# A conditioned decoder layer on one core: u and the spatial gates in token-major seven-product blocks

## The chip, the cores and the metric

The kernel runs on one core of a Trainium2 chip. The core has a matrix engine (PE, with its weight loads shown as PEld), a vector engine (DVE), a scalar engine (ACT), GpSimd (POOL) and a queue engine (SP), and 16 DMA engines that move data between the main memory and the on-chip buffer. Transfers are issued by SP; those that add into their destination are issued by POOL. Results of PE go to PSUM, eight banks of 128 partitions by 512 numbers. The metric is the time of one execution in microseconds of the device, lower is better.

## The reference

One layer works on 512 tokens of 2048 channels. The token matrix is normalised and modulated by a conditioning vector, and one projection gives everything that the two mixers need:

```python
proj = h @ w_in[l]
q_lat, kv_lat, k_rope, z_mla, u, v, z_sgu, g_mla, g_sgu = split_cols(proj, IN_SPLITS)
...
y_mla = causal_mla_attention(q_nope, q_rope, k_nope, k_rope, v_mla) * jax.nn.silu(z_mla)
mixed = jnp.einsum('gts,bnsgd->bntgd', ws, vc) + b_spatial.T[None, None, :, :, None]
y_sgu = u * mixed.reshape(B, S, SGU_WIDTH) * jax.nn.silu(z_sgu)
merged = jax.nn.sigmoid(g_mla) * y_mla + jax.nn.sigmoid(g_sgu) * y_sgu
x = x + gate[:, None] * (merged @ w_out[l])
return rmsnorm(x, final_norm_g)
```

`u`, `v`, `z_mla`, `z_sgu`, `g_mla`, `g_sgu` are 2048 channels wide each, 16 heads (or groups) of 128. In the spatial gating, `v` is normalised, cut into four chunks of 128 tokens, and for each group g multiplied by a lower triangular 128 x 128 matrix over the tokens of a chunk. The product of u, the mix, silu(z_sgu) and sigmoid(g_sgu) is called T below. All arithmetic is fp32.

## The kernel before

**Precision.** Each fp32 operand is split into a high and a low part (`hilo`, line 145: a cast by ACT, a subtraction by DVE), and each product is three matmuls, high by high, low by high, high by low. A weight tile of 128 x 1024 numbers (512 KB) is fetched raw, split, and used from one of three pairs of buffers (w0, w1, w2).

**Order of the stages.** First the latent columns (w1, w2: the low-rank q and kv latents and one 128-column head of z, g and u each), then 1088 of the v columns and one head of z by plain products (the loop over `steps`), then the first 1024 columns of v as a block of seven products (`V7`, 28 slots), then the other heads of z, g, u, s (= z_sgu) and t (= g_sgu) as 38 pairs of heads (`PAIRS`, 266 slots), then attention head by head, then the output projection.

**Seven products.** The product of a token half by a channel half is done after Winograd, with seven products for eight. The token sides are sums of the activations, made once (s1, s2, s4, and one that overwrites half of hh/hl). The weight sides are sums of raw weight tiles: B12 (called kept) plus B11, plus B22, minus B11 ("11b", `v_t3`), plus B21.

- In the *v block* the tokens are stationary and the weights stream, 512 columns at a time, so the result comes out token-major (128 tokens by 512 channels). A slot is one product over a quarter of the channels: 12 matmuls of 512 columns (lines 1422 to 1424). Four weight tiles are kept, and three buffers (raw4, raw5, raw6) take the passing ones in turn. Where sums are made by DVE, it is `v_sum` and `v_t3`; the last four sums (B21) are made by accumulating transfers on POOL's queue (line 901).
- In the *pairs* the weights are stationary and the tokens stream, 256 at a time, and the result is channel-major (128 channels by 512 tokens). A slot is one product over all eight channel tiles: 24 matmuls of 256 columns, or, for two of the seven, 8 of 512 and 8 of 256 (lines 1443 to 1447). Weight tiles are contiguous rows of 4 KB. Of a pair's four sums, DVE makes one and accumulating transfers three (`transfer`, line 722, issued in line 728); DVE makes more in the first and the last pair.

**A slot's order.** `on(s, phase, f)` puts work on slot s, in the order FIRST, EVAC, GATE, SPLIT, BACK, then PE's matmuls, then MISC and LOAD. The weights of slot g are split in slot g - 2. `place` finds, from slot s on, the first with room in DVE's budget, which is written down by `spend`: at most 3.2 us in a slot and 5.566 in two neighbours. Loads are issued in order by SP, accumulations in order by POOL, and each waits there until its buffer is free.

**The spatial mix.** For each group `v_load` fetches v token-major from a scratch in main memory, `sgu_scale` and `sgu_split` scale and split it, and `sgu_mix` multiplies with v stationary and the 256-wide high and low spatial weights streaming (lines 998 and 999), eight matmuls, which gives channel-major results in two banks. `sgu_out` (line 1002) puts in the gain and the broadcast bias and leaves it in the tile `bs[g]`; the pairs' gates (`gate_op`, line 827) then multiply u, s and t into it, and T is stored channel-major, one 256 KB tile a head.

**Other work of the pair stage.** The rotary tables (`rope_make`), the products of the shift with w1 and w2 that correct the early latents (`share`, 52 pieces of 256 KB, two accumulators in turn), and the normalisation of the latents (`lat_sq`, `lat_norm`), which fetches each of ten tiles twice.

**Attention.** `fetch(h)` loads T and the gate g of a head ahead of time. After the scores, the softmax, the transposes of the probabilities (line 1607) and the product with v, `merge_a` (line 1629) multiplies the result by g; its deferred second half adds T and splits the sum. PSUM banks go round in a ring of seven.

Of the kernel before, what the change touches and what calls it, by code (L numbers as in the profile page):

```python
# [20 lines left out]
P = 128  # L21
D = 2048
S = 512
# [40 lines left out]
class Stream:  # L64
# [17 lines left out]
    def dma_to(self, i):  # L82
        i = min(i, len(self.src) - 1 if self.limit is None else self.limit)
        while self.n_dma <= i:
# [7 lines left out]
            (self.first if k == 0 else self.nc.sync).dma_start(t[:, :n], ap)  # L92
# [29 lines left out]
def trunk_layer(ctx, tc, xT, xn, c, vecs, pos, wada, w1, w2, wv, wv3, wv4, wh, wh15, wq, wqr, wk, wvv, wo, wsT, bsp, gfin, out,  # L122
# [91 lines left out]
    gate_row = scratch("gate_row", [KC, P])  # L214
    cact_d = scratch("cact_d", [1, D])
# [7 lines left out]
    out_d = {t: [scratch(f"{t}_d{i}", [8, P, S]) for i in range(2)] for t in "gt"}  # L223

    lat = [nt(latp.p, [P, S], F32, f"lat{i}") for i in range(13)]
# [14 lines left out]
    g2 = [ws.add(w2[k], 640) for k in range(KC)]  # L240
# [9 lines left out]
    for cg, i in steps:  # L250
        if cg == "z":
            gb.append(ws.add(wh[H - 2, 0, i], GW))
# [236 lines left out]
    def half_of(tags, j):  # L489

        if j % 2 == 0:
            halves_[tags, j // 2] = nt(latp.p, [P, S], F32, tags[j // 2])
# [41 lines left out]
    def evac_v(n, cg, ps):  # L534
# [6 lines left out]
        else:  # L541
            t = nt(latp.p, [P, S], F32, "lat10" if n == 2 else "lat11" if cg == 1 else "lat6")
# [16 lines left out]
    def v_kept(i):  # L559
        p, tag = kept_at[i]  # L560
        kept[i] = nt(p(), [P, GW], F32, tag)
        DMA.dma_start(kept[i], wv[1][i])

    def v_pass(what, i):

        n = len(passing)
        t = passing[what, i] = nt(c1[0].p, [P, GW], F32, ("raw6", "raw4", "raw5")[n % 3])
        g, half = {"11": (0, 0), "11b": (0, 0), "21": (0, 4), "22": (1, 4)}[what]
        DMA.dma_start(t, wv[g][half + i])

    def v_sum(what, i):
        tt(kept[i], kept[i], passing[what, i], ALU.add)

    def v_t3(i):
        t = passing["11b", i]
        tt(t, kept[i], t, ALU.subtract)

    def v_split(g):
        p, i = V7[g]
        t = kept[i] if p in (6, 2, 4) else passing[{1: "11", 7: "22", 3: "11b", 5: "21"}[p], i]  # L580
        pl, tag = [(wp, "w1"), (wp, "w0"), (c1[0].p, "w2")][g % 3]
        vparts[g] = hi, lo = nt(pl, [P, GW], F32R, tag + "h"), nt(pl, [P, GW], F32R, tag + "l")
        hilo(hi, lo, t)

    for at_, f, *a in ((20, v_pass, "11", 0), (21, v_kept, 0), (22, v_pass, "11", 1), (23, v_kept, 1), (24, v_kept, 2),
# [1300 lines left out]
```

## Time and profile before

| | |
|---|---|
| median of three runs | 1594.26 us (1593.98 to 1595.37) |
| the profiled execution | span 1591.8 us from the first to the last instruction; no other time is given for it, and the median stands 2.5 us above it |
| granted PE clock, mean | 0.998 |
| v block | 259.49 to 335.78 us |
| pairs | from 335.78 us to about 1100 us |
| DMA | 335.35 MB, 211 GB/s on the mean |
| POOL's accumulating transfers | 60.30 MB, 21.6% of 16 engines' span |

A row of groups has the line, the engine, the operation, output and inputs, the shape, the count, and then the busy time, the mean of one in ns and the idle time before. A row of a timeline has the start, the duration, the engine and the operation, and in brackets the idle time before it and what ended it. A matmul's duration holds its passage through the array, so the pace of PE is read from starts and not from durations. A row of windows has the stretch, its length, busy time of PE, PEld, DVE, ACT and POOL with counts, the granted clock, the busy share of the DMA engines and GB/s. A row of a queue has packets, MB and the share of 16 engines' time.

### The profile page before, as it was taken

How to read it: one execution, taken by the hardware profiler on the slowest of the kernel's cores; microseconds unless marked ns; L12 is line 12 of the kernel's file. 1: busy time of each engine (PE TensorE's matmuls, PEld its weight loads, DVE VectorE, ACT ScalarE, POOL GpSimd, SP SyncE). 2: the span in 40 equal slices, each digit the busy share in tenths (PEclk: the TensorE clock that was granted, in tenths of full speed). 3: DMA queues.
4: the chain of work that ended last, by engine and by line, in shares of the span. 5: the costliest groups of instructions: out<-in, count | busy, mean ns of one | idle time of the engine just before them, and what ended most of it. 6: DMA issues, size and time to landing. Idle time of an engine off the chain costs nothing.

```text
span 1591.8 us, 25847 instructions
## 1 busy us (share of the span) xinstructions
PE 1579.7 (99%) x10107; PEld 1446.7 (91%) x10107; DVE 1225.3 (77%) x1831; ACT 766.4 (48%) x1271; POOL 108.4 (7%) x132
## 2 busy tenths in 40 slices
PE   9999999999999999999999999999999999999997
PEld 8888999889999999999999999999888898888886
DVE  8989788767877887787877777777788887866763
ACT  4443335555555454454545645645655555532332
POOL 0000000000111111111111111112000000000000
PEclk9999999999999999999999999999999999999999
DMA  9978566678799998889988879889422322339822
GB/s 384 358 290 317 199 185 216 179 221 223 204 235 244 244 260 227 219 241 237 232 210 241 232 205 265 221 216 224 147 83 87 102 90 86 97 135 387 289 88 106
DMA packets 124781, 335.35 MB, mean 211 GB/s; under 512 B 14298, under 2 KB 35826, under 8 KB 117874
## 3 DMA queue, kind: packets, MB, share of 16 engines
q1 hardware_dynamic: 106066, 272.88, 48.8%
q0 software_dynamic: 18448, 60.30, 21.6%
q8 instruction: 79, 1.29, 0.3%
q10 hardware_dynamic: 144, 0.52, 0.1%
q14 instruction: 44, 0.35, 0.1%
HBM read 309.45 MB, written 24.20 MB: 210 GB/s over the span
## 4 chain that ended last, share of the span: by engine, by line
PE 93%; DMA 2%; DVE 2%; ACT 1%; issue 1%; SPq 0%; DVEq 0%; ACTq 0%
PE ps L1447 15%; PE ps L142 14%; PE ps L143 14%; PE ps L141 14%; PE ps L1445 10%; PE ps L1446 10%; PE ps L1443 8%; PE ps L1424 2%; PE ps L1423 2%; PE ps L1422 2%; PE ps L1607 1%; PE ps L1570 1%; PE ps L1571 1%; DMA wsr<-in_wsT 1%; PE ps L998 1%
## 5 line engine op out<-in xcount | busy, mean ns | idle before, releaser
L1445 PE MATMUL ps<-hh,w2h 128*128 128x256 f32 x408 | 115.9, 284 | 0.0
L1445 PE MATMUL ps<-hh,w0h 128*128 128x256 f32 x408 | 115.6, 283 | 0.0
L1446 PE MATMUL ps<-hl,w2h 128*128 128x256 f32 x408 | 115.4, 283 | 0.0
L1446 PE MATMUL ps<-hl,w0h 128*128 128x256 f32 x408 | 115.4, 283 | 0.0
L1447 PE MATMUL ps<-hh,w0l 128*128 128x256 f32 x408 | 115.4, 283 | 0.0
L1447 PE MATMUL ps<-hh,w2l 128*128 128x256 f32 x408 | 115.4, 283 | 0.0
L1445 PE MATMUL ps<-hh,w1h 128*128 128x256 f32 x400 | 113.6, 284 | 0.0
L1446 PE MATMUL ps<-hl,w1h 128*128 128x256 f32 x400 | 113.2, 283 | 0.0
L1447 PE MATMUL ps<-hh,w1l 128*128 128x256 f32 x400 | 113.1, 283 | 0.0
L129 DVE TENSOR_TENSOR lat<-ps,lat 128x256 f32<-128x256 f32 (+2 forms) x202 | 97.1, 485 | 19.7 <-ACT lat L146 8.3
L132 DVE SCALAR_TENSOR_TENSOR wada<-wada,cact 128x2048 f32<-128x2048 f32 x47 | 107.2, 2281 | 4.7 <-DMA wada<-in_wada 4.7
L129 DVE TENSOR_TENSOR w2l<-raw,w2h 128x1024 fp32r<-128x1024 f32 x63 | 77.1, 1223 | 34.8 <-ACT w2h L748 30.9
L111 ACT CAST w1h<-wraw 128x1024 fp32r<-128x1024 f32 (+3 forms) x65 | 54.6, 841 | 99.0 <-PE ps L143 42.3
L111 ACT CAST w0h<-wraw 128x1024 fp32r<-128x1024 f32 (+3 forms) x66 | 60.4, 915 | 80.6 <-PE ps L143 29.9
L112 DVE TENSOR_TENSOR w0l<-wraw,w0h 128x1024 fp32r<-128x1024 f32 (+3 forms) x66 | 69.1, 1047 | 29.1 <-ACT w0h L111 28.9
L728 POOL DMA_DIRECT2D wraw<-in_wh x67 | 59.3, 939 | 448.3 <-DVE w0l L129 168.8
L141 PE MATMUL ps<-hh,w1h 128*128 128x512 f32 x226 | 89.7, 397 | 0.0
L129 DVE TENSOR_TENSOR w0l<-wraw,w0h 128x1024 fp32r<-128x1024 f32 x46 | 56.3, 1224 | 42.4 <-ACT w0h L748 40.0
L142 PE MATMUL ps<-hl,w1h 128*128 128x512 f32 x226 | 88.3, 391 | 0.5 <-DVE hl L132 0.5
L143 PE MATMUL ps<-hh,w1l 128*128 128x512 f32 x226 | 88.1, 390 | 0.0
L129 DVE TENSOR_TENSOR w1l<-raw,w1h 128x1024 fp32r<-128x1024 f32 x51 | 62.4, 1224 | 26.7 <-ACT w1h L748 23.5
L112 DVE TENSOR_TENSOR w1l<-wraw,w1h 128x1024 fp32r<-128x1024 f32 (+3 forms) x65 | 62.4, 960 | 26.0 <-ACT w1h L111 25.0
(410 smaller groups left out, 5298.3 us busy)
## 6 DMA issues: line engine op xcount, KB each, us to landing
raw<-in_wh SPq DMA_DIRECT2D x105, 512.0 KB, 6.3
wada<-in_wada SPq DMA_DIRECT2D x47, 1024.0 KB, 7.3
wraw<-in_wh POOLq DMA_DIRECT2D x67, 512.0 KB, 7.1
wraw<-in_wh SPq DMA_DIRECT2D x45, 512.0 KB, 7.2
raw<-in_wh POOLq DMA_DIRECT2D x42, 512.0 KB, 8.4
wraw<-in_wo SPq DMA_DIRECT2D x32, 512.0 KB, 5.0
half<-in_w SPq DMA_DIRECT2D x35, 256.0 KB, 5.7
raw<-in_wv SPq DMA_DIRECT2D x17, 512.0 KB, 3.9
```

The source lines that it names most:

```text
L111: self.nc.scalar.copy(hi[:, :n], raw[:, :n])
L112: self.nc.vector.tensor_tensor(out=lo[:, :n], in0=raw[:, :n], in1=hi[:, :n].bitcast(F32), op=ALU.subtract)
L129: DVE.tensor_tensor(out=out, in0=in0, in1=in1, op=op)
L132: DVE.scalar_tensor_tensor(out=out, in0=in0, scalar=scalar, in1=in1, op0=op0, op1=op1, **kw)
L141: PE.matmul(ps, ah, bh, start=start, stop=False)
L142: PE.matmul(ps, ah, bl, start=False, stop=False)
L143: PE.matmul(ps, al, bh, start=False, stop=stop)
L728: q_.dma_start(t, wh[h, n, q // 10 - 1], **eng)
L1443: PE.matmul(open_bank[k, "z"], wH[:, sl], both_parts[p](c), start=st, stop=False, skip_group_check=True)
L1445: PE.matmul(ps, wH[:, sl], xh, start=st, stop=False, skip_group_check=True)
L1446: PE.matmul(ps, wH[:, sl], xl, start=False, stop=False, skip_group_check=True)
L1447: PE.matmul(ps, wL[:, sl], xh, start=False, stop=sp, skip_group_check=True)
```

## The change

The 24 pairs that hold u, s and t become six blocks of the v block's form, 28 slots each, between the v block and the pairs; 14 pairs of z and g are left. A block has two column groups of 512 channels, four heads of one kind each.

- **Blocks and their weights.** `BLOCKS` lists them. `fill` gathers a weight tile from four heads: 256 numbers (1 KB) of each head's row, so a tile is 128 x 4 pieces of 1 KB; for the group with head 15 a second transfer brings that head from another array in pieces of 512 B. PE reads the moving operand as four runs of 128 (`p (h k w) -> p k h w`). Per block four tiles are kept and 16 pass; the B22 and the B21 sums are accumulating transfers, eight a block (also in the v block), B11 and B12 minus B11 are made by DVE. The next block's first tiles are fetched in the last nine slots of the one before.
- **Evacuation.** `t_copy`, `t_sub`, `t_add` move a quarter (two tiles of 128 x 512) at a time into six double tiles d0 to d5 that take the place of the single tiles lat0 to lat11. `squash` then applies Silu (s) or Sigmoid (t) to 1024 numbers a partition in one ACT instruction; `t_gate` multiplies it into u.
- **Mix.** v is multiplied by the gain (a row broadcast from main memory), the spatial weight is stationary, v streams: three matmuls of 512 columns into one bank, token-major. `sgu_out` is one operation for each token half, adding the bias per token and multiplying into u.
- **T** is stored token-major, eight tiles of 512 KB, fetched in pieces of 512 B, and turned in attention by four transposes a head (`turn`), with the add moved from the deferred half of the merge to the front.
- **Budget.** DVE's budget in `place` is 3.0 and 5.25 us in the blocks.
- **Moved.** The rotary tables, the shares and the mixes begin in block 1 instead of pair 0. The shares run one accumulator after another, each stored and fetched again before it is turned. Latent tiles are fetched once. The head of z that was done by plain products is now in w2's granules and head 14 of g is done by plain products in its place.

```diff
-PAIRS = [((t, h), (t, h + 1)) for h in range(0, 14, 2) for t in TYPES]
-PAIRS[:0] = [(("g", 14), ("u", 14))]
-PAIRS += [((t, 14), (t, 15)) for t in "st"]
+PAIRS = [((t, h), (t, h + 1)) for h in range(0, 14, 2) for t in "zg"]
+BLOCKS = [("v", 0, "v", 1)]
+for c_ in (0, 2):
+    BLOCKS += [("u", c_, "s", c_), ("t", c_, "u", c_ + 1), ("s", c_ + 1, "t", c_ + 1)]
...
+    def fill(q_, t, b, g, i, **kw):
+        ty, c = BLOCKS[b][2 * g:2 * g + 2]
+        if ty == "v":
+            q_.dma_start(t, wv[c][i], **kw)
+            return
+        n, half, o = TYPES.index(ty), i // 4, i % 4 * 2 * P
+        t = t.rearrange("p (h x) -> p h x", h=4)
+        hs = slice(4 * c, min(4 * c + 4, H - 1))
+        q_.dma_start(t[:, :hs.stop - hs.start], wh[hs, n, half][:, :, o:o + 2 * P].rearrange("h p x -> p h x"), **kw)
+        if hs.stop < 4 * c + 4:
+            src = w2[2 * i:2 * i + 2][:, :, S:].rearrange("k p w -> p k w")
+            if ty != "u":
+                src = wh15[i].rearrange("p (k t w) -> p k t w", k=2, t=2)[:, :, n - 3]
+            q_.dma_start(t[:, 3].rearrange("p (k w) -> p k w", k=2), src, **kw)
...
+    def v_add(b, g, i):
+        fill(nc.gpsimd, kept[b, i], b, g, 4 + i, accum_op=ALU.add)
...
-            return own > 3.2 or own + max(a, b) > 5.566
+            return own > (3.2 if s >= 0 else 3.0) or own + max(a, b) > (5.566 if s >= 0 else 5.25)
...
+    n_v = len(V7)
+    at_block = [n_v * (b - len(BLOCKS)) for b in range(len(BLOCKS))]
+    for b, V in enumerate(at_block):
...
+        sums_ = [(V - 2 + 2 * i, GATE, v_sum, b, "11", i) for i in range(0 if b else 1, 4)]
+        sums_ += [(V + s, GATE, v_t3, b, i) for i, s in enumerate((13, 14, 16, 17))]
...
+        loads = [("22", (1, 3, 5, 8)), ("11b", (10, 12, 14, 15)), ("21", (16, 17, 18, 19))]
+        if b + 1 < len(BLOCKS):
+            loads += [("11", (21, 23, 25, 27))]
+            block_events += [(V + 19 + 2 * i, LOAD, v_kept, b + 1, i) for i in range(4)]
...
+        block_events += [(V + 2 * i, LOAD, v_add, b, 1, i) for i in range(4)]
+        block_events += [(V + 15 + i, LOAD, v_add, b, 0, i) for i in range(4)]
...
+    def squash(key):
+        ACT.activation(held[key], held[key], AF.Silu if key[0] == "s" else AF.Sigmoid)
...
+        on(V + 7, EVAC, t_copy, al, p1, "y")
+        on(V + 8, EVAC, t_copy, br_, z6, "z")
+        on(V + 15, EVAC, t_copy, bl, u2, "y")
+        on(V + 18, EVAC, t_sub, bl, "z", True)
+        on(V + 20, EVAC, t_sub, br_, "y", False)
+        on(V + 27, EVAC, t_add, al, "w")
+        on(V + n_v, EVAC, t_copy, ar, c21, "y_before")
...
+    def sgu_mix(g):
+        wh_, wl_ = sgw["w"][:, 0], sgw["w"][:, 1]
+        vh, vl = (v.rearrange("p n w -> p (n w)") for v in sgw["hl"])
+        sgw["ps", g] = ps = bank()
+        mm3(ps, wh_, wl_, vh, vl, True, True)
...
+                    PE.matmul(ps[t].rearrange("p (h w) -> p h w", h=4), xh[:, tk], wH[:, k], start=st, stop=False, skip_group_check=True)
+                    PE.matmul(ps[t].rearrange("p (h w) -> p h w", h=4), xl[:, tk], wH[:, k], start=False, stop=False, skip_group_check=True)
+                    PE.matmul(ps[t].rearrange("p (h w) -> p h w", h=4), xh[:, tk], wL[:, k], start=False, stop=sp, skip_group_check=True)
...
+        DMA.dma_start(vt[h].rearrange("p (n w) -> p n w", n=NB),
+                      t_d[h // 4][:, :, h % 4 * P:(h % 4 + 1) * P].rearrange("n p w -> p n w"))
...
+    def turn(h):
+        ps = bank()
+        for n in range(NB):
+            tk = slice(n * P, (n + 1) * P)
+            PE.transpose(ps[:, tk], vt[h][:, tk], ident)
+        return ps
...
+    def merge_a(h, ps, turned_):
         m = nt(tp, [P, S], F32, "sig", bufs=3)
         tt(m, ps, gt[h], ALU.mult)
+        tt(m, m, turned_, ALU.add)
...
+        tps = turn(h)
         ops = pv(h, {**pa, **pb, **pc})
-        merge_a(h, ops)
+        merge_a(h, ops, tps)
```

More of the change, by code (lines that the diff above doesn't have):

```diff
@@ L828, in gate_op, with sigmoid @@
         box = {}
[L829 to L833 removed]
+        def sigmoid():
+            box["s"] = sig()
+            ACT.activation(box["s"], src, AF.Sigmoid)
+        on(s, GATE, sigmoid)
         def op():
```

495 lines of the change are left out of this document (268 added, 227 removed).

## The prediction

> **What bounds the kernel now.** I read the page first, then the engine table by windows, the groups of waits with the matrix engine as the one that waits, the timeline of single engines, and the transfer queues by window.
>
> ```profile
> span 1591.8 us, 25847 instructions
> PE 1579.7 (99%) x10107; PEld 1446.7 (91%) x10107; DVE 1225.3 (77%) x1831; ACT 766.4 (48%) x1271; POOL 108.4 (7%) x132
> ```
> ```profile
> 700.00:800.00 100.00, 100.00 (x761) 96.25 (x760) 78.91 (x113) 50.10 (x74) 12.89 (x15) 1.00 0.90 231
> 1200.00:1300.00 100.00, 100.00 (x592) 89.54 (x591) 79.90 (x167) 51.64 (x112) 0.00 (x0) 1.00 0.29 90
> ```
> ```profile
> PE ps L375 <- POOL mask L180: 1.1, 1, 1.1
> PE ps L1447 <- DVE w0l L129: 0.7, 1, 0.7
> PE ps L142 <- DVE hl L132: 0.5, 1, 0.5
> ```
>
> PE is busy 99% of the span, at a granted clock of 1.00 in the pair stage (700 to 800 us) and in attention (1200 to 1300 us). The waits of PE on other engines shown here, the three largest, are 2.3 us in all. So time comes out of PE's instruction stream alone: an edit is worth what it adds to or takes from that stream, and costs whatever new wait it makes PE take. The second fact is the last pair of columns: in the pair stage the 16 DMA engines are 0.90 busy, in attention 0.29. DVE has a fifth free, ACT half.
>
> **PE's stream: pairs against blocks.** Both forms already run in this trace: the v block (28 slots) and, right behind it, the pairs.
>
> ```profile
> 259.49 0.39 PE L1422 MATMUL ps<-w1h,hh 128*128 128x512 f32 x1
> 335.78 0.28 PE L1445 MATMUL ps<-hh,w0h 128*128 128x256 f32 x1
> 338.66 0.40 PE L1443 MATMUL ps<-s,w2h 128*128 128x512 f32 x1
> 352.95 0.39 PE L1443 MATMUL ps<-s,w0h 128*128 128x512 f32 x1
> ```
>
> The first row is where the block's first slot begins, the second where the first pair slot begins: 76.29 us for 28 slots, 2.725 us each (12 matmuls of 512 columns). The next two bound the pair slots: the first, with 24 matmuls of 256 columns, takes 338.66 - 335.78 = 2.88 us, and the six up to 352.95 take 17.17 us; a seventh of 2.88 gives 20.05 for a pair, 2.864 us a slot. The same columns are streamed, in fewer instructions. 24 pairs leave (168 slots), six blocks of 28 come (168 slots): 168 x (2.864 - 2.725) = **23.4 us off**.
>
> **Spatial mixes.**
>
> ```profile
> 359.65 0.28 PE L998 MATMUL ps<-whl,lat 128*128 128x256 f32 x1
> 359.77 0.22 PE L999 MATMUL ps<-whl,lat 128*128 128x128 f32 x1
> 359.83 0.34 PE L998 MATMUL ps<-whl,lat 128*128 128x256 f32 x1
> 360.52 0.45 PE L1443 MATMUL ps<-s,w1h 128*128 128x512 f32 x1
> 311.30 0.39 PE L1422 MATMUL ps<-w0h,hh 128*128 128x512 f32 x1
> 311.53 0.39 PE L1423 MATMUL ps<-w0h,hl 128*128 128x512 f32 x1
> ```
>
> A group's mix takes 360.52 - 359.65 = 0.87 us now. It becomes three matmuls of 512 columns, each 0.227 us (28 slots of 12 above; the last two rows are two neighbours), 0.68 us. 16 x 0.19 = **3.0 us off**.
>
> **T turned by TensorE.** Attention gets four transposes a head.
>
> ```profile
> 645.57 0.28 PE L1447 MATMUL ps<-s,w1l 128*128 128x256 f32 x1
> 645.70 0.60 PE L1088 MATMUL ps<-ident,rx 128*128 128x128 f32 x4
> 646.05 0.36 PE L1445 MATMUL ps<-hh,w0h 128*128 128x256 f32 x1
> 646.25 0.28 PE L1446 MATMUL ps<-hl,w0h 128*128 128x256 f32 x1
> ```
>
> From the matmul before four such transposes to the second one behind, 0.68 us pass, where two 256-column matmuls alone take 2 x 0.12; so four cost 0.44 us. 16 heads: **7.0 us on**; two small ones for the bias rows, 0.2 us, too. The Trainium skill (TensorE: Matmul & The Clock Gate, Part 4) gives about 275 ns for a transpose in a kernel; 64 of them would be 17.6 us and the sum 10.6 us worse. The trace has the four closer together than that, and I go by the trace.
>
> The add of T moves: it was a SBUF add in the deferred half of the merge, now it reads PSUM at once, ahead of the next head's mask add.
>
> ```profile
> 1224.70 0.69 DVE L129 TENSOR_TENSOR sig<-ps,g 128x512 f32<-128x512 f32 x1 [0.54 <-PE ps L143]
> 1225.89 0.30 DVE L129 TENSOR_TENSOR ps<-ps,mask 128x128 f32<-128x128 f32 x1 [0.51 <-PE ps L1571]
> ```
>
> Between the merge's multiply and the mask add DVE waits 0.51 us for PE in this head. The extra 0.69 us fits but for 0.2, and PE then has a projection to run before it needs the softmax: 0. The seven-bank ring gains one bank a head, read by that same add before it comes round: 0. If the cover went, 16 x 0.69 = 11 us.
>
> **Sum of PE's stream:** -23.4 - 3.0 + 7.0 + 0.2 = **-19.2 us**. One thing in it is not in the trace: the blocks read their moving operand in four runs of 128 with a stride. Low end 0, since a block's matmul stays one instruction of 512 columns; high end, if each run cost what a 128-column matmul does (359.83 - 359.77 = 0.06), 4 x 0.06 - 0.227 = 0.013 us for each of 2016 matmuls, 26 us. I take 0: same count of columns and instructions as the v block.
>
> **What could make PE wait: the weights' transfers.** The bytes are the same (28 x 512 KB per block or four pairs). Two things change. Rows of 4 KB become pieces of 1 KB (a quarter of the partition for each of four heads); and four pairs' 12 accumulating transfers (the POOL queue, reading and adding) become 8, so 16 plain ones become 20. Prices, from queue totals in four stretches:
>
> ```profile
> q1 hardware_dynamic: 7650, 31.66, 89.6%
> q0 software_dynamic: 576, 2.10, 55.8%
> q0 software_dynamic: 2234, 1.29, 57.4%
> q1 hardware_dynamic: 3315, 1.81, 39.7%
> ```
>
> First row, 0 to 90 us, rows of 4 and 8 KB: 0.896 x 90 x 16 engine-us for 31.66 MB, so 512 KB occupy the 16 engines 1.34 us. Second, 296 to 316 us, four accumulations of 4 KB rows: 0.558 x 20 / 4 = 2.79 us each. Third and fourth, 1073 to 1090 us, where nearly all is in 512 B pieces: 3.97 us per 512 KB accumulated, 1.95 plain. 1 KB lies between; linear in the piece's size it is **3.30 and 1.60 us** (estimates from these rows). A block then needs 20 x 1.60 + 8 x 3.30 = 58.4 of 76.3 us, against 16 x 1.34 + 12 x 2.79 = 54.9 of 80.2 for four pairs. Beside it run v, share and T transfers. On average it still fits; in one place it does not. The v block shows it, since the new blocks keep its order:
>
> ```profile
> 299.00 0.86 POOL L901 DMA_DIRECT2D wraw<-in_wv  x1 [1.65 <-ACT w0h L146]
> 298.81 1.22 DVE L129 TENSOR_TENSOR w0l<-raw,w0h 128x1024 fp32r<-128x1024 f32 x1 [0.35 <-ACT w0h L146]
> 307.24 1.23 DVE L129 TENSOR_TENSOR raw<-wraw,raw 128x1024 f32<-128x1024 f32 x1 [0.20 <-DMA raw<-in_wv]
> 309.65 1.23 DVE L129 TENSOR_TENSOR w0l<-raw,w0h 128x1024 fp32r<-128x1024 f32 x1 [1.19 <-ACT w0h L146]
> ```
>
> The buffer of the fourth "11b" weight is free at 300.03; it lands at 307.24, and DVE waits for it. Its subtraction, cast and low part end at 310.88; PE needs them at 311.30. So 0.42 us are to spare, and two accumulations and two loads share the engines ahead of that landing. At the new prices these take 2 x 0.51 + 2 x 0.26 = 1.54 us more: the subtraction waits on DVE, the low parts queue behind it, and PE waits for them 1.1 us. The third accumulation and the first "21" load, needed next, add 0.77: 1.9. A share or v load (256 KB) ahead in SP's queue costs half of 1.34 to half of 1.95 when it falls into these four slots; DVE's budget is full there, so few do: 0.3 on average. **S = 2.2 us a block, 13.2 us in six.** Bounds: 0 (4 KB prices) and, at 512 B prices, 2 x 1.18 + 2 x 0.61 - 0.42 + 1.79 = 5.0.
>
> The Trainium skill (DMA: Bandwidth & Descriptors, Specifications) has 512 B as enough for line rate. By that 1 KB pieces cost nothing and the sum stays near -19 us (second rival below). In the rows the 512 B pieces took 1.4 times as long per byte, so I go by the rows.
>
> **The other engines.** DVE, a block: 28 low parts and 8 sums of 1.22, six half-wide subtractions of 0.69, 48 us; 16 gates of 1.22 and 16 groups of about 2.9 (six narrower operations, by width) add 66 / 6 = 11: 59 of 76, as full as now (78.91 of 100). Shares and the rotary tables go into the rest, earlier than before; they hide until the budget is used up. On ACT, gates become 1024 wide, and Silu stands beside Sigmoid:
>
> ```profile
> L832 ACT ACT_TABLE_LOAD x4 | 5.1, 1283 | 0.1
> 299.94 1.27 ACT L914 COPY t<-ps 128x512 f32<-128x512 f32 x2 [1.17 <-PE ps L1424]
> 324.88 1.05 ACT L146 CAST w2h<-raw 128x1024 fp32r<-128x1024 f32 x1 [1.67 <-PE ps L1423]
> 325.96 1.23 DVE L129 TENSOR_TENSOR w2l<-raw,w2h 128x1024 fp32r<-128x1024 f32 x1 [1.50 <-ACT w2h L146]
> ```
>
> If the two need different tables, a block's end has two copies (1.27), a table load (1.28) and a gate (about 1.05, as a cast of that width) ahead of a cast. A cast begins two slots (5.45 us) before its product and needs 2.3 with the low part: 3.1 us to spare for 3.6 in front, 0.5 us at four block ends; I take half of that, 1.0 us, since a table load is not certain; bounds 0 and 5. SP's queue issues the same number of weight loads (the last heads' in two parts), POOL 48 accumulations for 72; who waits for them is counted in S. The lat tiles are loaded once instead of twice, accumulators are stored and fetched again, T loads in attention come in 512 B pieces where DMA is 0.29 busy: 0, covered by that slack.
>
> **Forecast:** 1591.8 - 19.2 + 13.2 + 1.0 = 1586.8 us of span. The runs' median (1594.26) is 2.5 us above this execution's span, so 1586.8 + 2.5 = **1589 us**, 0.3% faster.
>
> **Rivals.** (1) *Transfers bind, slower.* One mechanism, S: the change loses from 3.0 us a block (18.2 / 6) and is slower by over 0.2% (3.2 us, about what the measurement tells from nothing) from 3.6. For it: 0.90 busy already, the 5.0 above, FIFO order behind share loads. Against: accumulations fall by a third, and the six-slot windows have room. At S = 5: 1594.3 - 18.2 + 30 = 1606 us. (2) *No new wait:* PE's sum alone, 1594.3 - 19.2 = 1575 us; for it the single wait of 0.7 us on a low part, in a pair stage at 0.90 busy; against it the 0.42 us above. (3) *No change that can be told:* S from 2.5 to 3.6, 1591 to 1597; it needs one share load more in each window than I count. (4) *The strided operand costs,* the gain is not there: up to 1589 + 26 = 1615 us.
>
> **Numbers.** Forecast (S from 1.2 to 2.5, 1583 to 1591): 0.35. Rival 2: 0.20. Rival 3: 0.17. Rival 1: 0.23. Rival 4: 0.05. Faster 0.55, same 0.17, slower 0.28. The range 1576 to 1606 leaves out rival 4, half of rival 1's tail and the lowest end of rival 2; the likeliest case alone is 1583 to 1591.
>
> **What would show it.** Right: block slots 2.73 us apart on PE in the clean stretches, three matmuls per mix, four transposes a head at 0.44 us, attention 7 us longer; once per block, two thirds through, PE idle 1 to 3 us for a low part whose subtraction waited for a raw weight's transfer. Rival 1: several such waits per block, DMA at 0.95 and more. Rival 2: no PE wait over 0.5 us. Rival 4: more than 2.73 us per block slot with no releaser named. I am wrong if PE waits in the blocks for PSUM evacuations or for DVE's own backlog instead, or in attention for T.

## The result, and the profile after

The changed kernel takes 1605.59 us in the median of four runs (1603.99 to 1606.07), the kernel before beside it 1594.82 us (1593.98 to 1599.67): 1.006 times as long, 95% interval 1.0045 to 1.0075. The forecast was 1589 us. The page of its profiled execution begins:

```profile
span 1604.4 us, 22537 instructions
PE 1570.6 (98%) x8461; PEld 1361.5 (85%) x8461; DVE 1202.6 (75%) x1719; ACT 769.4 (48%) x1220; POOL 117.4 (7%) x118
```

PE is busy for 9.1 us less than before, where its stream was forecast 19.2 us shorter, and it stands idle for 33.8 us in place of 12.1, so the span is 12.6 us longer: PE now waits, and part of what it saves is lost to a slower pace behind the waits (below). Cut at starts of PE instructions (attention from the first transposes of the probabilities to the last), the two executions compare so, in us:

| stretch | before | after | difference | predicted |
|---|---|---|---|---|
| start to the v block | 259.49 | 261.33 | +1.84 | 0 |
| v block | 76.29 | 76.81 | +0.52 | 0 |
| u, s, t, z, g up to the first projection of attention | 782.04 | 781.13 | -0.91 | -12.0 |
| from there to the first transposes | 29.11 | 32.97 | +3.86 | 0 |
| attention | 268.51 | 275.62 | +7.11 | +7.0 |
| to the last matmul | 167.59 | 168.03 | +0.44 | 0 |
| to the end | 8.77 | 8.51 | -0.26 | 0 |

The groups of waits with PE as the one that waits, longest totals first, show what is new (line 1533 to 1535 are a block's matmuls, 1555 a pair's, `d` the double tiles into which PSUM is emptied):

```profile
PE ps L1533 <- DVE d L132: 4.9, 4, 1.4
PE ps L1533 <- ACT w2h L149: 2.4, 2, 2.0
PE ps L429 <- ACT hh L420: 2.2, 1, 2.2
PE ps L1533 <- ACT w1h L149: 2.0, 2, 1.0
PE ps L1555 <- DVE d L132: 1.9, 1, 1.9
PE ps L1535 <- DVE w0l L132: 1.8, 4, 0.5
PE ps L1535 <- DVE w2l L132: 1.7, 3, 0.6
PE ps L1535 <- DVE w1l L132: 1.4, 3, 0.5
```

Two kinds stand there: waits for a weight's high or low part (w0, w1, w2), and waits for DVE to have read a PSUM bank that PE wants to write again (`d`). (The row of line 429 belongs to the kernel's first 20 us.) For the blocks I measured every slot from the start of its first matmul to that of the next slot's, and took off 2.72 us and 0.23 for each mix matmul inside. What is left is lost. In the changed kernel that is 24.9 us in the six blocks, 4.1 a block, and 22.6 of it in three slots: 6.2 in slot 18, 8.6 in slot 19, 7.8 in slot 20 (a wait at the beginning of a slot counts to the one before). Only 15.0 us of it is PE standing idle; the other 10 are matmuls that start further apart than 0.23 us, mostly right behind a wait. The v block is 0.65 us longer than 28 slots of 2.72, without any wait: 0.49 of that stands in slots 16 and 17, at the two small operations for the bias rows, which the prediction had at 0.2.

Block 1 shows both kinds. First the timeline of DVE, then that of PE:

```profile
389.47 1.23 DVE L132 TENSOR_TENSOR raw<-wraw,raw 128x1024 f32<-128x1024 f32 x1 [2.74 <-DMA raw<-in_wh]
391.94 1.23 DVE L132 TENSOR_TENSOR w2l<-raw,w2h 128x1024 fp32r<-128x1024 f32 x1 [1.24 <-ACT w2h L149]
...
398.37 1.22 DVE L132 TENSOR_TENSOR w0l<-raw,w0h 128x1024 fp32r<-128x1024 f32 x1 [2.09 <-ACT w0h L149]
399.51 0.28 DVE L132 TENSOR_TENSOR half<-half,rx 128x128 f32<-128x128 f32 x1
...
400.35 0.29 DVE L132 TENSOR_TENSOR rx<-rx,half 128x128 f32<-128x128 f32 x1
400.56 1.28 DVE L132 TENSOR_TENSOR d<-d,ps 128x512 f32<-128x512 f32 x2
```

```profile
391.96 0.50 PE L1533 MATMUL ps<-w2h,hh 128*128 128x512 f32 x1 [1.97 <-ACT w2h L149]
393.22 0.80 PE L1535 MATMUL ps<-w2l,hh 128*128 128x512 f32 x1 [0.53 <-DVE w2l L132]
...
401.39 0.47 PE L1533 MATMUL ps<-w0h,hh 128*128 128x512 f32 x1 [1.39 <-DVE d L132]
```

The subtraction for the fourth 11b weight waits 2.74 us for its transfer, the cast and the low part follow, and PE waits 1.97 and 0.53 us for them: the place that the prediction named. Eight microseconds later PE waits 1.39 us for the y bank: its two subtractions (`t_sub` of slot 20, at 400.56) stand on DVE behind a late low part and four small operations of the rotary tables. The low part, which waited 2.09 us, came late because its cast did; on ACT the cast stood, without a pause, behind a table load and a gate:

```profile
395.04 1.28 ACT L1032 ACT_TABLE_LOAD   x1
396.33 1.06 ACT L1032 ACTIVATE d<-d 128x1024 f32<-128x1024 f32 x1
397.30 1.04 ACT L149 CAST w0h<-raw 128x1024 fp32r<-128x1024 f32 x1
```

### The profile page after: what moved, and what is told of

Its sections match the earlier page's. It is cut to its first block, busy times and chain, and to the rows that moved or that the text cites. A ratio compares the mean times of both kernels' runs of the same rounds, so it can differ in the third digit from the quotient of the medians.

```text
span 1604.4 us, 22537 instructions
## 1 busy us (share of the span) xinstructions
PE 1570.6 (98%) x8461; PEld 1361.5 (85%) x8461; DVE 1202.6 (75%) x1719; ACT 769.4 (48%) x1220; POOL 117.4 (7%) x118
## 4 chain that ended last, share of the span: by engine, by line
PE 84%; DMA 7%; DVE 5%; ACT 2%; issue 1%; SPq 0%; DVEq 0%; ACTq 0%
PE ps L146 14%; PE ps L144 14%; PE ps L145 14%; PE ps L1535 8%; PE ps L1533 8%; PE ps L1534 8%; PE ps L1559 5%; DMA raw<-in_wh 5%; PE ps L1558 4%; PE ps L1557 4%; PE ps L1555 3%; PE ps L1724 1%; DVE w0l L132 1%; DVE w2l L132 1%; DVE raw L132 1%
## 5 line engine op out<-in xcount | busy, mean ns | idle before, releaser
L132 DVE TENSOR_TENSOR w0l<-raw,w0h 128x1024 fp32r<-128x1024 f32 x62 | 75.8, 1223 | 35.2 <-ACT w0h L149 26.2
L132 DVE TENSOR_TENSOR d<-ps,d 128x256 f32<-128x256 f32 (+2 forms) x130 | 72.4, 570 | 17.1 <-ACT d L149 13.1
L144 PE MATMUL ps<-hh,w0h 128*128 128x512 f32 x198 | 78.0, 394 | 1.0 <-ACT d L900 1.0
L146 PE MATMUL ps<-hh,w0l 128*128 128x512 f32 x198 | 77.4, 391 | 0.5 <-DVE w0l L115 0.5
L145 PE MATMUL ps<-hl,w0h 128*128 128x512 f32 x198 | 77.2, 390 | 0.0
L149 ACT CAST w1h<-raw 128x1024 fp32r<-128x1024 f32 x45 | 47.3, 1051 | 57.2 <-PE ps L1534 37.1
L149 ACT CAST w0h<-raw 128x1024 fp32r<-128x1024 f32 x44 | 46.2, 1050 | 53.7 <-PE ps L1534 23.6
L144 PE MATMUL ps<-w0h,hh 128*128 128x256 f32 (+2 forms) x224 | 67.8, 303 | 0.0
L146 PE MATMUL ps<-w0h,hl 128*128 128x256 f32 (+2 forms) x224 | 67.5, 301 | 0.0
L145 PE MATMUL ps<-w0l,hh 128*128 128x256 f32 (+2 forms) x224 | 67.4, 301 | 0.0
```

The source lines that it names most:

```text
L132: DVE.tensor_tensor(out=out, in0=in0, in1=in1, op=op)
L144: PE.matmul(ps, ah, bh, start=start, stop=False)
L145: PE.matmul(ps, ah, bl, start=False, stop=False)
L146: PE.matmul(ps, al, bh, start=False, stop=stop)
L149: ACT.copy(hi, src)
```

## The experiments

Each edit is against the changed kernel unless it says otherwise. "Lost" is what the six new blocks lose in one profiled execution, counted as above; the columns of slots leave out what is under 0.15 us.

| kernel | time, us | lost | slot 18 | slot 19 | slot 20 | v block |
|---|---|---|---|---|---|---|
| changed | 1605.59 | 24.9 | 6.2 | 8.6 | 7.8 | 0.65 |
| rows4k | 1592.07 | 12.2 | 1.0 | 4.9 | 5.0 | 0.64 |
| dve21 | 1614.42 | 29.8 | 0 | 0.7 | 12.4 | 1.85 |
| noshare | 1601.25 | 21.7 | 4.3 | 8.3 | 7.9 | 1.53 |
| sigm | 1604.60 | 23.3 | 6.0 | 8.8 | 7.5 | 1.07 |
| spread | 1606.61 | 23.6 | 6.2 | 6.5 | 9.0 | 1.46 |
| order | 1600.97 | 21.6 | 6.1 | 8.3 | 2.9 | 0.68 |
| key | 1602.92 | 25.6 | 6.8 | 8.1 | 8.2 | 1.14 |
| v1k | 1609.22 | 26.9 | 5.8 | 7.5 | 9.6 | 2.18 |
| order_key | 1596.72 | 20.8 | 7.7 | 9.8 | 1.5 | 0.69 |
| all4 | 1584.58 | 9.2 | 2.0 | 3.8 | 0 | 1.22 |
| all4_dve1 | 1586.57 | 9.4 | 0 | 0.8 | 7.7 | 0.99 |
| noshare4k | 1589.12 | 8.5 | 0.6 | 2.1 | 4.4 | 1.07 |
| all4_noshare | 1581.24 | 3.9 | 1.0 | 2.5 | 0 | 0.72 |

**rows4k: rows of 4 KB for the blocks' weights.**

```diff
-        q_.dma_start(t[:, :hs.stop - hs.start], wh[hs, n, half][:, :, o:o + 2 * P].rearrange("h p x -> p h x"), **kw)
...
+        q_.dma_start(t, wb[TYPES.index(ty) - 2, c, i], **kw)
```

> The weights of the six new blocks come from a copy in device memory in which each weight's 128 partitions are rows of 4 KB, in place of four pieces of 1 KB from four heads; nothing else changes. The blocks lost 23.5 us in waits (six lengths of 83.1, 80.6, 80.6, 83.2, 81.9, 82.0 us against 76.3 for 28 slots of 2.725, less 10.9 for the mixes within them). Theory A (the transfers of slots 13 to 20 are late for their piece size, and the late subtraction of the y bank and the half clock behind it follow from that): 512 KB accumulated go back from 3.41 to 2.79 us and plain from 1.76 to 1.34, the stalls fall from 3.9 us a block to 0.5 or less, and the time falls by 20 to 23 us, to 1583 to 1586 us. Theory B (the shares' loads in front in SP's queue, and DVE full by its own work): two accumulations and two loads ahead of the fourth 11b get 2.1 us cheaper, but the rest of 1.8 us a block stays: 1592 to 1594 us. Theory C (the table loads on ACT and DVE's backlog, transfers hidden anyway): no more than 2 us, 1603 to 1606 us.

1592.07 us, 0.9976 of the kernel before (0.9966 to 0.9986). The loss falls by 12.7 us, 2.1 a block: the number of theory B. The queues' rows, first the changed kernel in block 1 (338.14 to 421.22 us), then this one (338.0 to 417.2):

```profile
q1 hardware_dynamic: 12003, 11.71, 47.3%
q0 software_dynamic: 4224, 4.19, 32.8%
```
```profile
q1 hardware_dynamic: 5039, 11.80, 42.6%
q0 software_dynamic: 1152, 4.19, 29.5%
```

An accumulation of 512 KB occupies the 16 engines for 0.328 x 83.08 / 8 = 3.41 us in pieces of 1 KB (forecast 3.30) and 0.295 x 79.2 / 8 = 2.92 us in rows of 4 KB; a plain 512 KB takes 1.76 us (forecast 1.60) and 1.50. So half of the loss is the pieces' size, and the other half is there at 4 KB too, where the prediction had set the lower end of S at nothing. (The edit also does away with head 15's pieces of 512 B; blocks 1 to 3, which have none beside them, gain 2.2 us each on the mean.)

**dve21: the four B21 sums of a new block made by DVE.**

```diff
-        block_events += [(V + 15 + i, LOAD, v_add, b, 0, i) for i in range(4)]
+        if b:
+            block_events += [(V + 19 + 2 * i, GATE, v_sum, b, "21", i) for i in range(4)]
+        else:
+            block_events += [(V + 15 + i, LOAD, v_add, b, 0, i) for i in range(4)]
```

> In the six new blocks the four accumulating transfers of the window (slots 15 to 18, weight W21 added in place by the POOL queue) are replaced by four sums on DVE from the raw W21 tile, which is loaded anyway; pieces stay 1 KB. It takes 4 x 3.41 us of 16 engines out of slots 15 to 20 of each block and puts 4 x 1.22 us on DVE in slots 19 to 25. Theory A (late transfers): the fourth 11b and the first 21 land in time, the stalls fall from 3.9 us to about 1 us a block, 1605.6 - 17 = 1588 us. Theory B (DVE full by its own work and its backlog is what PE waits for): DVE gets 4.9 us more a block just where it is late; the stalls grow by 2 to 5 us a block, 1618 to 1635 us. Theory C (ACT's table loads): no change in the window, 1604 to 1612 us.

1614.42 us (1.0111, 1.0096 to 1.0126). Both theories see their part: slots 18 and 19, the late transfers, are cured (14.8 to 0.7 us), but slot 20 loses 12.4 us and slots 21 to 27 some 14. The first groups of PE's waits:

```profile
PE ps L1536 <- DVE d L132: 9.2, 4, 2.6
PE ps L1538 <- DVE w2l L132: 3.0, 6, 0.5
```

DVE has a quarter of the span free and no room just there.

**noshare: most of the shares left out.**

```diff
-    shares = [(q, (k,), w1[k][:, q * S:(q + 1) * S]) for q in range(2) for k in range(KC)]
-    shares += [(2, (k,), w2[k][:, :S]) for k in range(KC)]
+    shares = [(q, (k,), w1[k][:, q * S:(q + 1) * S]) for q in range(2) for k in (0, KC - 1)]
+    shares += [(2, (k,), w2[k][:, :S]) for k in (0, KC - 1)]
```

> Left out: 42 of the 52 share steps (a load of 256 KB and one or two DVE operations of 0.7 us each, which add up shift times w1 and w2), so the bias of the latents is not the full sum. All transfers of the blocks' weights and their pieces stay. Theory A (the blocks' own transfers): the stalls fall by little, the 0.3 us a block that the prediction gave to share loads, at most 1 us; the chain of shares, bias, latents and key ends earlier, so the entry to attention goes back from 33.0 to 29.1 us: 1605.6 - 2 - 4 = 1600 us. Theory B (share loads in front in SP's queue and DVE full by shares): stalls fall below 1 us a block, 1605.6 - 18 - 4 = 1584 us. Theory C (ACT): only the entry, 1602 us.

1601.25 us (1.0028, 1.0017 to 1.004), near theory A in sum, but the sum hides a contrast. The ten steps left ran from 441 to 531 us, closer together than before, in block 2 and the beginning of block 3. Block 2 lost 6.4 us for 3.1; blocks 3 to 6, with no share near their slots 13 to 20, lost 9.4 us for 15.6. So shares beside the window cost about 1.5 us a block, five times the 0.3 of the prediction. The run takes away a share's load and its DVE operations together and does not tell which of them costs; in block 4 of all4 (below) DVE's share operation ends at 623.32 us and DVE then stands idle for 1.91 us until a weight lands, so there a landing is late and not DVE. The entry to attention went back by 0.9 us only: the key is made as late as before, since the planner still puts it into the last slots.

**sigm: Sigmoid in place of Silu.**

```diff
-        ACT.activation(held[key], held[key], AF.Silu if key[0] == "s" else AF.Sigmoid)
+        ACT.activation(held[key], held[key], AF.Sigmoid)
```

> Silu of the s gates becomes Sigmoid (so the s gates are not the reference's), which takes away the switch between the two activation tables at the ends of the blocks and leaves everything else. Theory A: each table load of 1.28 us that goes is worth what it adds behind the late cast, 0.2 to 0.5 us in four blocks: 1603.5 to 1605 us. Theory C (the table load in front of the cast is what makes the low part late): stalls fall by 1.3 to 2 us in the blocks that have an s gate near their end, four or five of them: 1597 to 1600 us.

1604.60 us, 1.0 us less than with Silu, and the loss in the blocks 1.6 us less. That is the size forecast for the table loads, though 1 us is inside the spread of the runs (1604.29 to 1607.81) and 1.6 is close to what two executions of one schedule differ by (spread, 1.3). The edit takes away three of the five table loads at the gates and brings one at another place (412.8 us); the one in block 1 stays, at 397.1 us, and with it that block's loss in slot 20 (1.6 us in both kernels). So theory C falls for the loads that went, and the part of ACT in block 1 was not tried.

**spread: the four accumulations written two slots apart.**

```diff
-        block_events += [(V + 15 + i, LOAD, v_add, b, 0, i) for i in range(4)]
+        block_events += [(V + 15 + (2 * i if b else i), LOAD, v_add, b, 0, i) for i in range(4)]
```

> Pieces stay 1 KB. In the six new blocks the four accumulations of W21 start at slots 15, 17, 19, 21 in place of 15, 16, 17, 18 (their sums are not needed before slots 19, 21, 23, 25). So one to two of them, 3.4 us of all 16 engines each, leave the stretch in which the last two 11b weights and the first 21 weight come. In the changed kernel PE loses, over six blocks, 6.2 us in slot 18, 8.6 in slot 19 and 7.8 in slot 20. Theory A (late transfers in that stretch make the waits of slots 18 and 19): slot 18 falls below 1.5 us in all, slot 19 to about 5.5 (what it has with 4 KB rows), slot 20, if it is a consequence, by 2: 1605.6 - 10 = 1595 us; without the consequence 1598. Theory B (DVE's own backlog): no change, 1604 to 1606 us.

1606.61 us: nothing. The timeline of POOL in block 2 says why, first the changed kernel (block 2 from 421.22 us), then this one (from 421.69):

```profile
468.62 1.27 POOL L587 DMA_DIRECT2D wraw<-in_wh  x1 [4.82 <-DVE raw L132]
474.00 1.28 POOL L587 DMA_DIRECT2D wraw<-in_wh  x1 [4.10 <-issue]
```
```profile
469.09 1.27 POOL L587 DMA_DIRECT2D wraw<-in_wh  x1 [4.82 <-DVE raw L132]
474.50 1.28 POOL L587 DMA_DIRECT2D wraw<-in_wh  x1 [4.14 <-issue]
```

These are the third and the fourth accumulation, and their issues are the same 47.40 and 52.8 us behind the block's start, in both kernels about 0.5 us behind the end of the subtraction that reads the kept tile (468.10 and 473.47 us in the changed kernel). A later slot in the program's order held nothing back here, since POOL's queue had nothing else in it. The edit changed no transfer, so it tells nothing of either theory; it is also a measure of how far two executions of one schedule differ (1.3 us in what the blocks lose, 0.8 in the v block).

**order: the y bank's subtractions ahead of the planned work of slot 19.**

```diff
         spend(s, us)
+        if -6 * len(V7) <= s < 0 and s % len(V7) == 19:
+            s += 1
         on(s, BACK, f, *a)
```

> Transfers unchanged. DVE work that the planner puts into slot 19 of a block (parts of the spatial groups, gates, shares) is written behind the two subtractions that empty the y bank, in slot 20, in place of ahead of them. If the wait at the end of slot 20 (7.8 us over six blocks, PE waiting for DVE to have read the y bank) is made by what stands ahead of these subtractions in DVE's queue, it falls to 2 us or less in all and the time by 5 to 6 us, to 1600 us. If it is only a consequence of the late low parts before it (theory A alone), it stays, and the time is 1604 to 1606 us.

1600.97 us (1.003, 1.0019 to 1.0042), near the forecast for the order on DVE: slot 20 falls from 7.8 to 2.9 us. 3.8 us come back in slots 21 to 23, nearly all in two blocks, where PE, no longer held in slot 20, meets the next late weight; the row of ACT in block 3:

```profile
565.37 1.05 ACT L149 CAST w0h<-raw 128x1024 fp32r<-128x1024 f32 x1 [4.13 <-DMA raw<-in_wh]
```

Slots 18 and 19 stay. So the order on DVE is a cause of its own and not a consequence of the late weights.

**key: the rotary key made four slots earlier.**

```diff
-            s_ = place(s_ + 1, 0.95, lat_recip, q)
+            s_ = place(s_ + (q == 0), 0.95, lat_recip, q)
...
-            s_ = place(s_ + 1, 0.75, lat_norm, i)
+            s_ = place(s_ + (i == lo_), 0.75, lat_norm, i)
...
+            return own > (3.2 if s >= 38 else 3.2 if s >= 0 else 3.0) or own + max(a, b) > (5.7 if s >= 38 else 5.566 if s >= 0 else 5.25)
```

> Blocks unchanged. In the pair stage, behind slot 38, the planner may put the latents' reciprocals and products closer together (the one after in the same slot where DVE's budget allows, the budget of two neighbouring slots 5.7 us in place of 5.566), so the rotary key is made in slots 92 to 94 in place of 96 to 98 of 98. If the longer entry to attention (33.0 us against 29.1) comes from the four copies of the key (2.51 us on ACT) that now stand in front of the latents' splits, the entry goes back to 29 to 30 us and the time to 1602 us. If it comes from the late weights of the first projections (ACT waits 2.9 us for one), it goes back by 1 us at most: 1604.5 us. DVE gets a little fuller in the pair stage: up to 1 us lost there.

1602.92 us, with runs from 1599.41 to 1606.53, so the gain in time is not sharp; the trace is clearer: the entry takes 29.38 us for 32.97. The timeline of ACT around it, in the changed kernel with what PE waited for, and in this one:

```profile
1118.55 2.51 ACT L1431 COPY d<-rx 32x512 f32<-32x512 f32 x4
1121.08 1.95 ACT L1461 ACTIVATE hh<-b,vec 128x512 fp32r<-128x512 f32 x3
1121.86 0.50 PE L144 MATMUL ps<-hh,w1h 128*128 128x512 f32 x1 [0.34 <-ACT hh L1461]
1125.82 0.50 PE L144 MATMUL ps<-hh,w0h 128*128 128x512 f32 x1 [1.04 <-ACT d L900]
```
```profile
1104.59 2.51 ACT L1431 COPY d<-rx 32x512 f32<-32x512 f32 x4
```

The four copies that swap the key's halves stood in front of the splits of the latents, and everything behind them on ACT was late: the splits, the last pair's evacuation, the first weights' casts. Moved, they delay nobody.

**v1k: the v block's weights in pieces of 1 KB too.**

```diff
-            q_.dma_start(t, wv[c][i], **kw)
+            q_.dma_start(t.rearrange("p (h x) -> p h x", h=4), wv[c][i].rearrange("h p x -> p h x"), **kw)
```

> The changed kernel, with the weights of the v block too in pieces of 1 KB in place of rows of 4 KB. The v block has the same order of transfers as the six new blocks, but none of their gates, groups and shares beside it; with 4 KB rows it loses 0.65 us (0.36 of it at slot 16). The prediction sized the piece effect from this block: the fourth 11b weight lands 1.54 us later against 0.42 us to spare, then 0.77 us more: 1.9 us in slots 18 and 19. If that model holds by itself, the v block loses 2.0 to 3.0 us and the time is 1607 to 1608 us; the new blocks' 3.9 us are then more for what runs beside them. If the model is too small (the engines are full there, so every transfer behind is late too), the v block loses 4 us or more. If pieces of 1 KB don't matter, 0.6 to 1 us.

1609.22 us. The v block loses 2.18 us, within the 2.0 to 3.0 of the model, but most of that is not the pieces' doing: 0.49 are the two bias-row operations, and 0.95 stand in slot 20, at a wait for the first 21 weight that kernels with 4 KB rows in this block show too. Here is the wait in v1k, then the same one in dve21:

```profile
319.70 0.51 PE L1535 MATMUL ps<-w2l,hh 128*128 128x512 f32 x1 [0.53 <-DVE w2l L132]
```
```profile
317.78 0.50 PE L1538 MATMUL ps<-w2l,hh 128*128 128x512 f32 x1 [0.53 <-DVE w2l L132]
```

Kernels that leave the v block's own transfers alone lose 0.64 to 1.85 us there, so the piece effect in it is 0.3 to 1.5 us, less than the model's 1.9; slot 19, with 0.54 us for 0.25 at most elsewhere, is all that v1k has alone. A block with nothing beside it bears small pieces; the new blocks' 4.1 us need the company.

**order_key: the edits of order and of key, as shown above; pieces of 1 KB.**

> 1 KB pieces; the y bank's subtractions ahead of the planner's work of slot 19 (alone 1601.0 us), and the key made earlier in the pair stage (alone 1602.9). Both waits are on different places; if they add, 1605.6 - 4.6 - 2.7 = 1598.3 us, still above the kernel before: what is left, some 20 us of stalls in slots 18 and 19 and behind, is then the transfers' share. If one was noise, 1600 to 1603 us.

1596.72 us (1.0005, 0.9995 to 1.0016): level with the kernel before; the gains add, and 1.6 us more, which is inside the spread of the runs (1594.76 to 1600.41).

**all4: the edits of rows4k, spread, order and key together.**

> 4 KB rows, accumulations at slots 15, 17, 19, 21, the y bank's subtractions first, and the earlier key, together. 4 KB rows alone gave 1592.1 us with 12.2 us of stalls left in the blocks (2 in slot 18 and others, 5 in slot 19, 5 in slot 20). If the late transfers and the order on DVE are the whole cause, 2 to 4 us of stalls stay, and with 3.5 us from the entry the time is 1592 - 9 - 3.5 = 1579 to 1582 us, 1% below the kernel before. If there is a third cause (the chain of subtraction, cast and low part on DVE and ACT is too long for the slots 18 and 19 whatever lands when), 5 us stay in slot 19: 1585 us.

1584.58 us, 0.9928 of the kernel before (0.991 to 0.9947), so this version beats both. The groups of PE's waits, longest first:

```profile
PE ps L144 <- ACT hh L420: 1.7, 1, 1.7
PE ps L1529 <- DVE w0l L132: 1.5, 3, 0.5
PE ps L1529 <- DVE w2l L132: 1.3, 3, 0.5
```

No wait for `d` is left in the blocks, and slot 20 loses nothing; 5.8 us stay in slots 18 and 19, nearer to the third cause's 5 than to the 2 to 4 hoped for.

**all4_dve1: all4, and the first B21 sum of a block on DVE (the edit against all4).**

```diff
-        block_events += [(V + 15 + (2 * i if b else i), LOAD, v_add, b, 0, i) for i in range(4)]
+        block_events += [(V + 15 + (2 * i if b else i), LOAD, v_add, b, 0, i) for i in range(1 if b else 0, 4)]
+        if b:
+            block_events += [(V + 19, GATE, v_sum, b, "21", 0)]
```

> All four edits (1584.6 us, 9.2 us of stalls left, nearly all in slots 17 to 19), and of the four accumulations of W21 in a new block the first, which runs in the full stretch ahead of the fourth 11b weight, becomes a sum on DVE in slot 19. If the remaining wait is still the late landing in a stretch where the engines are full (0.94 to 1.03 busy), 4 KB accumulated, 2.8 us of 16 engines, leave it: the stalls of slots 18 and 19 fall to 3 us or less, 1584.6 - 5 = 1580 us. If it is the chain of subtraction, cast and low part, nothing changes there, and the sum costs up to 1 us a block in slot 20: 1585 to 1590 us.

1586.57 us: one accumulation less in the window cures slots 18 and 19 (5.8 to 0.8 us), which rules out the chain of subtraction, cast and low part, unchanged here, as their cause by itself, and the 1.22 us on DVE bring the y bank's wait back (7.7 us in slot 20).

```profile
PE ps L1529 <- DVE d L132: 5.5, 5, 1.3
```

**noshare4k: the edits of rows4k and noshare.**

> 4 KB rows, and 42 of the 52 share steps left out (the bias of the latents is not the full sum). The ten steps that are left run in the first two new blocks, so the last four have no share at all. Lost in those four blocks: changed kernel 15.6 us, 4 KB rows alone 9.0, shares left out alone 9.4. If pieces and shares are two separate loads on the same full engines, both gone leaves what neither makes, the y bank's wait of slot 20 (3.9 us with 4 KB rows in these blocks): 4 to 5 us in the four blocks, 1592.1 - 4.5 = 1587.5 us. If what is left with 4 KB rows has nothing to do with the shares, 8 to 9 us stay and the time is 1591 us.

**all4_noshare: those of all4 and noshare.**

> 4 KB rows, the y bank's subtractions first, the earlier key, and 42 of the 52 share steps left out (the bias of the latents is not the full sum). If pieces, shares and the order on DVE are the whole of what the new blocks lose beyond the v block, the last four blocks lose what the v block does, 0.65 us each, 2.6 us in all (6.4 with the shares in place), and the time is 1584.6 - 4 = 1580.5 us. If a further cause is left (gates and spatial groups on ACT and DVE, loads of v), 5 us or more stay in these four blocks: 1583 to 1585 us.

1589.12 us (1587.5 if pieces and shares are separate, 1591 if not) and 1581.24 us (1580.5 expected). Blocks 3 to 6 lose 5.0 us with 4 KB rows and no shares (9.0 with them; 4 to 5 expected) and 1.56 us when the order on DVE is mended too (2.6 expected), 0.00, 1.46, 0.10 and 0.00 each. Pieces, shares and order are thus nearly all of what these blocks lose; the 1.46 us in block 4 stay unexplained. Block 1, which has no share in any kernel, still loses 1.8 us; it has the rotary tables instead, and that was not tried.

**before_again: the kernel before, profiled a second time.**

> The kernel before, unchanged, profiled a second time. The v block began at 259.49 us in its first profile and at 261.2 to 263.3 us in those of the changed kernel and its variants, although nothing ahead of it was changed. If that is a difference between executions, it begins somewhere from 259.5 to 263.3 us here too; if the change causes it, at 259.5 again. 1594 to 1597 us.

1594.08 us; the v block begins at 259.71 us. In the changed kernel and the thirteen variants it begins between 261.2 and 263.8, so this is hardly chance. The difference is there by 18 us, where DVE runs the same instructions in both and waits for the second 1 MB of conditioning weights. The rows of DVE, before and after:

```profile
12.54 2.29 DVE L132 SCALAR_TENSOR_TENSOR wada<-wada,cact 128x2048 f32<-128x2048 f32 x1 [1.00 <-DMA wada<-in_wada]
```
```profile
14.36 2.29 DVE L135 SCALAR_TENSOR_TENSOR wada<-wada,cact 128x2048 f32<-128x2048 f32 x1 [1.86 <-DMA wada<-in_wada]
```

Why the same transfer lands later stays open.

## Why the prediction was wrong

- **Pairs against blocks, -23.4 us: right.** Of block 1, slot 0 begins at the first row and slot 18 at the second: 48.96 us, 2.72 each. The strided operand (rival 4) costs nothing.

```profile
338.14 0.39 PE L1533 MATMUL ps<-w0h,hh 128*128 128x512 f32 x1
387.10 0.39 PE L1533 MATMUL ps<-w0h,hh 128*128 128x512 f32 x1
```

- **Mixes, -3.0 us: right.** A slot with a mix takes 3.40 us, 0.68 more.
- **T turned by PE, +7.0 us: right.** Attention is 7.11 us longer; from the matmul before the four transposes to the second behind it is 0.90 us, less two of 0.23: 0.44 again. The moved add costs nothing. The two small operations for the bias rows took 0.49 us in place of 0.2, in the v block.

```profile
1155.88 0.40 PE L146 MATMUL ps<-hh,w1l 128*128 128x512 f32 x1
1156.11 0.60 PE L1750 MATMUL ps<-ident,b 128*128 128x128 f32 x4
1156.47 0.47 PE L144 MATMUL ps<-hh,d 128*128 128x512 f32 x1
1156.78 0.39 PE L145 MATMUL ps<-hl,d 128*128 128x512 f32 x1
```

- **The transfers, S = 2.2 us a block: the step that failed, and it decided the sign.** The place that it named was right. The size of what it priced, 1.9 us of piece effect, met the 2.1 us a block that rows4k takes off, but in part by luck: the prices are called linear in the piece's size, and 3.30 and 1.60 us are linear in the number of pieces (in the size they would be 3.80 and 1.86; measured were 3.41 and 1.76); in the v block alone the effect is 0.3 to 1.5 us (v1k); and of the 12.7 us that rows4k takes off, 8.9 are in slots 18 and 19, for which the 1.9 stands, and 2.8 in the y bank's slot 20. Wrong was the base to which it was added, "Bounds: 0 (4 KB prices)", read from the v block "since the new blocks keep its order". They keep the order of their own transfers, but not the company. With 4 KB rows they still lose 2.0 us each, by shares beside the window ("0.3 on average", measured about 1.5 at 1 KB and 1.0 at 4 KB, in blocks 3 to 6) and by the y bank, which the prediction did not cost at all: its "I am wrong if" names the wait, its sum has nothing for it. The block lost 4.1 us, over the 3.6 from which rival 1 is slower; rival 1 had the outcome and the order of size, but only half of its mechanism, since it put all on transfers. That its 1606 us stands beside the measured 1605.59 is luck: it is reckoned with S = 5, and the rest of the way here was the start and the entry to attention.
- **Rival 2, no new wait: wrong.** The Trainium skill (DMA: Bandwidth & Descriptors, Specifications), by which 512 B are enough for line rate, does not hold here: in block 1 a plain 512 KB occupied the engines for 1.76 us in 1 KB pieces and 1.50 in 4 KB rows, and from 1 KB to 4 KB the time fell by 13.5 us.
- **Table loads, +1.0 us: not contradicted.** Three loads fewer gave 1.0 us, inside the spread of the runs (sigm).
- **DVE's rest, "they hide until the budget is used up", 0: wrong.** The budget counts microseconds in a slot. It was kept, and PE still waited, because work that nobody waits for stood ahead of the two subtractions that free a bank (order, 4.6 us of time). In block 1 a low part that waited for ACT stood there too.
- **Entry to attention, moved shares and latents, 0: wrong by 3.9 us.** The chain that was moved ends later, and its last link met ACT where it had no slack (key gives 3.6 us of it back).

In sum: -12.0 us were forecast up to attention and -0.91 came; 10.7 of the 11.1 us between them are the 24.9 us lost in the blocks for 14.2 expected (13.2 and 1.0); with the entry (3.9), the start (1.8) and the v block (0.5) the forecast of -5.0 us of span became +12.6.

## What to carry to other kernels

A stretch that already runs is a good price list for one that copies its order, but only for the work inside it: list also what runs beside it on the same queues and engines in the copy, and price the window with that. When transfers are cheap on the mean and late in one place, look first at the size of their contiguous pieces, then at who else loads there; moving sums from a full transfer window to a vector engine with a quarter of its time free helped that window and cost more behind it. In an in-order queue an operation that frees a PSUM bank belongs ahead of all work that nobody waits for, and a budget by microseconds does not see to that.

## What the runs showed of the hardware

Two short waits close together went with a lowered clock of PE, but not each time. In block 1 PE waited 1.97 and 0.53 us within four microseconds; the next matmuls started 0.43 us apart instead of 0.23, for about 3 us. In block 5 it waited 1.00 and 0.53 us, and the same followed. In block 2 it waited 0.99 and 0.53 us, and the clock stayed at 1.00. The windows of the changed kernel (the granted clock stands ahead of the last two columns), two of block 1, at the second wait and behind it, then one of block 5 and one of block 2 behind theirs:

```profile
391.00:394.00 3.00, 1.51 (x4) 0.98 (x5) 2.06 (x3) 0.93 (x2) 1.28 (x1) 0.83 1.17 253
394.00:397.00 3.00, 3.00 (x10) 2.33 (x9) 1.59 (x2) 2.97 (x3) 0.00 (x0) 0.60 1.15 199
721.00:724.00 3.00, 3.00 (x9) 2.35 (x8) 0.57 (x1) 0.95 (x1) 0.00 (x0) 0.50 1.18 268
476.00:479.00 3.00, 3.00 (x12) 2.09 (x12) 1.70 (x3) 1.65 (x2) 0.00 (x0) 1.00 1.17 271
```

Slot 19 of block 1 lost 2.42 us for 0.53 us of waiting, and that of block 5 2.53 for 0.53, so where the clock falls such a wait is much dearer than its own length; in blocks 2, 4 and 6 a slot with a single wait of 0.53 us lost 0.93 to 1.00. What decides between the two was not found. The Trainium skill (TensorE: Matmul & The Clock Gate, Part 1) says that idle gaps above about 3.4 us are to be avoided; here no single wait in the blocks was above 1.97 us, and the clock fell behind two of them in two blocks of six. The same rows show the transfer engines' share at 1.15 to 1.18, where 1 would be all 16 busy for the whole stretch.
